# A hybrid encoder layer on one core: MLP operands of the second half in half-width pieces, early operands tied to the softmax, the survey spaced, reciprocal roots on VectorE

## Chip, cores and metric

One core of a Trainium2 chip runs the whole layer in one launch. The metric is device time in microseconds, from start to end of the program. The kernel before took 2134.22 us (median of 3 runs, 2132.43 to 2136.63).

## What is computed

One layer (x is 2048 tokens by 1024 channels, float32):

```python
h = rms_norm(x, norm1_g)
p = h @ w_in                       # 1024 -> 2560, shared by three groups
q, k, v = p[:512], p[512:1024], p[1024:1536]        # 8 heads of 64
q, k = rms_norm(q per head), rms_norm(k per head)
y_attn = softmax(q k^T / 8 + rel_bias) v            # own chunk of 64 and 8 chunks before
y_conv = gb * conv3_causal(gc * hin)                # 256 wide
y_pool = (trailing means over 2, 4, 8, 16 - u) @ pool_w * pool_scale
x = x + concat(y_attn, y_conv, y_pool) @ w_out
h2 = rms_norm(x, norm2_g)
x = x + square(relu(h2 @ w_mlp1)) @ w_mlp2          # 1024 -> 4096 -> 1024
```

The norm of a row is `x * rsqrt(mean(x*x) + 1e-6) * g`. All products are made from a high and a low part of each operand (three matmuls for one), so that float32 accuracy is kept.

## The kernel before, in words

**Four blocks, then two halves.** The first part goes over four blocks of 512 tokens (`block(b, prev_out)`, L374). A block projects q, k and v (`project`, L399), normalizes q and k (`normalize`, L435), and makes the first head pair's operands (`prep`, L453), which are moved by DMA, the keys by way of DRAM (L471, L480, L485), before the first score. Then comes its attention. The second part is the MLP, over two halves of 1024 tokens (`tb` 0 and 1), written as Strassen-like products: seven operands of the data (`OPS`, L329) against seven of the weights (`WORDER`, L49) for each of 64 units (L918). A unit is `up` (L939) or `down` (L965) and has 84 matmuls of 128x512; the order is four up, four down, four times for each half. In the first half the weights' operands are made on ACT, DVE and POOL (`weight_sums`, L812) one unit ahead and kept in DRAM; the second half only loads them (L907).

**Order.** In a block the attention is the main stream, and a side stream is woven into it (`weave`, L75): for every step of the attention 0.95 steps of the side (0.45 in block 0). The PE order is written out by that weaving (`ORDERED`, L44); all other instructions are placed by the framework's scheduler, on each engine and in each DMA queue, by its own timing model: an instruction is put where its inputs are ready and its engine is free, earlier code first. All DMAs go through the SP queue. The side stream (`side`, L770) is the output projection of the block before (`outproj`, L726), its row statistics (`stats`, L746), then the convolution and pooling (`convpool`, L644).

**The survey.** `pace` (L759) also takes a step of the survey (`survey`, L265) at the first two of every five side steps. A survey step issues the loads of two 128x512 tiles of MLP weights and squares, on ACT (L272), the two loaded one step before; four buffers serve them. `paced` (L261) ties a square in the schedule behind the last exponential of the attention that has been written by then; at run time no engine waits for it.

**Early operands.** The first half's seven data operands for each of four `k` (`early_operands`, L331) are made in block 3: 4 loads, 4 DVE products (L347), 7 casts on ACT (L353) with 7 DVE differences (L354), 4 POOL differences (L359 to L368) and 7 stores for each `k`. They need x2 of blocks 0 and 1 only. Their 28 steps stand in `side` behind the statistics, one at each step of `convpool`, and the last ones behind it.

**The second half's operands.** `prepare_spill` (L873) makes them in the MLP's first half, one `k` at each of the units 6, 10, 14 and 18 (`SPILLS`, L48): 2 + 4 loads, 4 DVE products (L869), the sums of `data_sums` (L835, 4 on POOL), 7 casts (L805) and 7 differences (L806), 7 stores (L876). Units 6 and 14 are down units, 10 and 18 up units.

**Roots.** `rsqrt` (L162) is a square root on ACT (L164), a reciprocal on DVE (L166) and one Newton step of four DVE instructions (L168 to L171). It is used three times in a block (rows, q, k) and once for the statistics of each block. The exponential (L549) and the square root need different tables on ACT, and a change of table is an instruction of its own, ACT_TABLE_LOAD.

## Time and profile before

| | |
|---|---|
| runs | 2134.22 us (2132.43 to 2136.63), 3 runs |
| profiled execution | 2131.85 us, span 2130.1 us |
| PE busy | 2040.0 us (96%), 11072 matmuls |
| DVE busy | 1339.8 us (63%) |
| ACT busy | 1019.6 us (48%) |
| POOL busy | 579.0 us (27%) |
| mean DMA rate | 188 GB/s |

The profile is one execution. In the windows view a line is a stretch in us from the span's start; after its length stand the busy time of each engine and the number of its instructions, then the TensorE clock that was granted (1.00 is 2.4 GHz, and a piece at the lower level, 1.2 GHz, counts half), the busy share of the 16 DMA engines and GB/s. In the timeline and the lines view, what stands in brackets or behind the bar is the idle time of that engine just before, and what ended it.

### The profile page before, as it was taken

To read this page: it belongs to the slowest core of one execution; us is meant where nothing else is said; L and a number is where in the kernel's file an instruction comes from. 1 tells how busy PE (TensorE), PEld (TensorE's weight loads), DVE (VectorE), ACT (ScalarE), POOL (GpSimd) and SP (SyncE) were. 2 spreads that over 40 slices of the span, in tenths; PEclk is the share of its full clock that TensorE was granted. 3 is DMA by queue.
4 is the path that set the end of the run, shared out by engine and by line. 5 is a ranking of instruction groups with operands and counts; after the bars stand their busy time and mean duration, and the time that the engine had idled before them with its cause. 6 is when DMAs were issued, how large, how long until landed. Compare 5 with 4: busy or idle time off the path is not lost.

```text
span 2130.1 us, 31726 instructions
## 1 busy us (share of the span) xinstructions
PE 2040.0 (96%) x11072; PEld 1255.2 (59%) x11072; DVE 1339.8 (63%) x2184; ACT 1019.6 (48%) x2036; POOL 579.0 (27%) x441
## 2 busy tenths in 40 slices
PE   8999998999899699999999999999999999999999
PEld 6777787878787588864444444444444444444444
DVE  6776566755679767757768789767743053353354
ACT  5565575747675455535656456356143151150330
POOL 1110012000212213144556456436422031130132
PEclk9999999999999899999999999999999999999999
DMA  9685688648866776483565565548733333333344
GB/s 336 204 258 192 201 270 246 224 139 273 254 211 208 233 209 180 157 327 121 170 221 183 185 201 188 178 160 295 250 116 100 103 101 102 103 95 109 100 152 150
DMA packets 219568, 399.70 MB, mean 188 GB/s; under 512 B 26000, under 2 KB 33296, under 8 KB 219408
## 3 DMA queue, kind: packets, MB, share of 16 engines
q1 hardware_dynamic: 219408, 397.68, 58.3%
q8 instruction: 87, 1.43, 0.3%
q14 instruction: 73, 0.60, 0.1%
HBM read 275.42 MB, written 105.38 MB: 179 GB/s over the span
## 4 chain that ended last, share of the span: by engine, by line
PE 38%; DVE 5%; POOL 3%; DMA 3%; issue 3%; ACT 2%; SPq 0%; POOLq 0%; DVEq 0%; ACTq 0%
PE b_d L855 21%; PE b_u L855 17%; DMA r_d<-w 1%; DVE ft_u L806 1%; POOL t1u L839 1%; DVE a_d L809 1%; DVE acc L976 1%; DVE s_d L809 1%; POOL r_d L824 0%; DVE x L869 0%; POOL s_d L822 0%; DVE a_u L809 0%; DMA rr<-r2d 0%; DMA xd<-yb 0%; ACT ft_u L805 0%
## 5 line engine op out<-in xcount | busy, mean ns | idle before, releaser
L855 PE MATMUL b_d<-ft_u,s_d 128*128 128x512 f16 x1152 | 264.1, 379 | 5.4 <-DVE ft_u L806 2.0
L855 PEld LDWEIGHTS <-s_d 128*128 128x128 f16 x1536 | 150.2, 98 | 188.1 <-issue 7.1
L855 PEld LDWEIGHTS <-s_u 128*128 128x128 f16 x1536 | 150.7, 98 | 186.2 <-issue 7.0
L855 PE MATMUL b_u<-zt,s_u 128*128 128x512 f16 x1152 | 257.3, 381 | 1.8 <-DVE u2u L958 1.0
L976 DVE TENSOR_TENSOR acc<-acc,b_d 128x512 f32<-128x512 f32 x176 | 119.2, 683 | 178.9 <-PE b_d L855 175.6
L855 PEld LDWEIGHTS <-a_u 128*128 128x128 f16 x1152 | 112.7, 98 | 146.3 <-issue 12.7
L855 PEld LDWEIGHTS <-a_d 128*128 128x128 f16 x1152 | 112.7, 98 | 142.5 <-issue 7.4
L855 PE MATMUL b_d<-fb_u,a_d 128*128 128x512 f16 x768 | 183.7, 379 | 3.5 <-DVE fb_u L806 1.7
L855 PE MATMUL b_u<-zb,a_u 128*128 128x512 f16 x768 | 176.6, 379 | 1.3 <-ACT u2u L945 1.3
L839 POOL TENSOR_TENSOR t1u<-u2u,c11u 128x512 f32<-128x512 f32 x32 | 44.0, 1376 | 442.8 <-ACT u2u L962 430.6
L159 PE MATMUL a<-wq,xg 128*128 128x512 f32 x384 | 155.0, 404 | 1.9 <-DVE wq L140 1.8
L158 PE MATMUL a<-wq,xg 128*128 128x512 f32 x384 | 144.6, 403 | 12.5 <-ACT wq L139 12.5
L160 PE MATMUL a<-wq,xg 128*128 128x512 f32 x384 | 153.6, 400 | 0.0
L549 ACT ACTIVATE sb<-sb,nm 128x640 f32<-128x640 f32 (+4 forms) x128 | 97.5, 762 | 110.7 <-DVE nm L543 109.3
L207 POOL TENSOR_TENSOR acc<-acc,sq 128x512 f32<-128x512 f32 x28 | 38.0, 1357 | 379.2 <-ACT sq L206 353.0
L543 DVE CUSTOM_DVE_ANT_0 sb<-s,b 128x640 f32<-128x640 f32 (+4 forms) x128 | 94.3, 737 | 64.6 <-PE s L540 64.0
L562 DVE SCALAR_TENSOR_TENSOR pp<-pt,pp 128x384 f16<-128x384 f32 (+1 forms) x224 | 101.9, 484 | 45.5 <-ACT pp L561 45.0
L139 POOL CAST wc<-rwc 128x512 fp32r<-128x512 f32 x64 | 40.7, 636 | 252.5 <-PE cp L160 109.1
L158 PE MATMUL o<-mix,wo 128*128 128x512 f32 x256 | 106.4, 416 | 1.3 <-ACT mix L641 1.0
L158 PE MATMUL cp<-xg,wc 128*128 128x512 f32 x256 | 106.7, 417 | 0.0
L945 ACT COPY u2u<-b_u 128x512 f32<-128x512 f32 x32 | 18.5, 577 | 179.9 <-PE b_u L855 176.8
L159 PE MATMUL cp<-xg,wc 128*128 128x512 f32 x256 | 101.5, 397 | 0.0
(270 smaller groups left out, 4389.3 us busy)
## 6 DMA issues: line engine op xcount, KB each, us to landing
rwq<-w_qkv SPq DMA_DIRECT2D x96, 256.0 KB, 3.2
p<-w1t SPq DMA_DIRECT2D x64, 256.0 KB, 4.6
rwc<-w_cp SPq DMA_DIRECT2D x64, 256.0 KB, 4.4
rwo<-w_out SPq DMA_DIRECT2D x64, 256.0 KB, 4.0
t<-w SPq DMA_DIRECT2D x64, 256.0 KB, 4.1
r_u<-w SPq DMA_DIRECT2D x64, 256.0 KB, 3.3
wd<-s_u SPq DMA_DIRECT2D x64, 256.0 KB, 2.4
r_d<-w SPq DMA_DIRECT2D x64, 256.0 KB, 3.0
```

The source lines that it names most:

```text
L139: (hi or sc.copy)(w[:, 0], raw)
L158: te.matmul(out, ah, bh, start=start, stop=False)
L159: te.matmul(out, ah, bl, start=False, stop=False)
L160: te.matmul(out, al, bh, start=False, stop=stop)
L207: gp.tensor_tensor(out=acc, in0=acc, in1=q, op=ALU.add)
L543: ve.tensor_tensor_reduce(out=sb[:, :nk].rearrange("p (e k) -> p e k", e=ne), in0=s[:, :ne, :hk], in1=bi[:, 640 - nk :].rearrange("p (e k) ...
L549: exps.append(sc.activation(sb[:, :nk], sb[:, :nk], AF.Exp, bias=nmx, scale=-1.0, accum_out=st["l"][:, i, j : j + 1]))
L562: ve.scalar_tensor_tensor(out=pp[:, 1, c0:c1], in0=pt[:, :n], scalar=PSC, in1=pp[:, 0, c0:c1], op0=ALU.mult, op1=ALU.subtract)
L809: ve.scalar_tensor_tensor(out=t[:, 1], in0=src, scalar=scale, in1=t[:, 0], op0=ALU.mult, op1=ALU.subtract)
L839: gp.tensor_tensor(out=t1, in0=b12, in1=b11, op=ALU.subtract)
L855: te.matmul(bank, w[:, a, q * P : (q + 1) * P], xs[q][:, c], start=start and q == 0 and i == 0, stop=q == n - 1 and i == 2, skip_group_che ...
L976: ve.tensor_tensor(out=a, in0=a, in1=bk, op=ALU.add)
```

## The change

Five edits, in one diff.

- `SPILLS` names eight units, all of them down units: 5 and 7, 12 to 15, 20 and 21. `prepare_spill` makes half of a `k`'s columns at each (256 of each 512), so the four `k` are done in eight pieces; loads, DVE, ACT and POOL instructions are 256 wide, and a store fills half of a row's columns.
- The four DVE products of the early operands are `paced`, as the survey's squares are.
- `side` interleaves the early operands with the whole side stream: one of their steps at each third step from the output projection on; those left over come at its end. The whole stream has 64 steps without them, so 21 of the 28 fall into it and 7 behind it.
- The survey's two steps in five side steps are the first and the fourth, not the first and the second.
- `rsqrt` has a form that needs no ACT: a shift and a subtraction on the integer bits, then three Newton steps of three DVE instructions, 11 in all. The old form stays for the rows, q and k of block 0.

```diff
-SPILLS = (6, 10, 14, 18)
+SPILLS = (5, 7, 12, 13, 14, 15, 20, 21)
...
-    def rsqrt(pool, a, n, tag):
+    def rsqrt_table(pool, a, n, tag):
...
+    def rsqrt(pool, a, n, tag, table=False):
+        if table:
+            return rsqrt_table(pool, a, n, tag)
+        h = pool.tile([P, n], I32, tag=tag + "h", name=tag + "h")
+        ve.tensor_scalar(h, a.bitcast(I32), 1, None, op0=ALU.arith_shift_right)
+        r = pool.tile([P, n], F32, tag=tag + "r", name=tag + "r")
+        ve.tensor_scalar(r.bitcast(I32), h, -1, 0x5F3759DF, op0=ALU.mult, op1=ALU.add)
+        t = pool.tile([P, n], F32, tag=tag + "t", name=tag + "t")
+        for _ in range(3):
+            ve.scalar_tensor_tensor(out=t, in0=r, scalar=-0.5, in1=r, op0=ALU.mult, op1=ALU.mult)
+            ve.tensor_tensor(out=t, in0=t, in1=a, op=ALU.mult)
+            ve.scalar_tensor_tensor(out=r, in0=t, scalar=1.5, in1=r, op0=ALU.add, op1=ALU.mult)
         return r
...
-                    ve.scalar_tensor_tensor(out=t, in0=t, scalar=g2s[:, kk : kk + 1], in1=rr[n], op0=ALU.mult, op1=ALU.mult)
+                    paced(ve.scalar_tensor_tensor(out=t, in0=t, scalar=g2s[:, kk : kk + 1], in1=rr[n], op0=ALU.mult, op1=ALU.mult))
...
-            rstd.append(rsqrt(sm, ms1, NT, "r1"))
+            rstd.append(rsqrt(sm, ms1, NT, "r1", b == 0))
...
-            f = rsqrt(sm, ss.rearrange("p t h -> p (t h)"), NT * H, "rq")
+            f = rsqrt(sm, ss.rearrange("p t h -> p (t h)"), NT * H, "rq", b == 0)
...
         def pace(steps):
             for n, _ in enumerate(steps):
-                if n % 5 < 2:
+                if n % 5 in (0, 3):
                     next(surveyed, None)
...
+        def main_side():
             yield from prev_outproj(weights)
             c = convpool()
             for _ in prev_stats():
                 next(c)
                 yield
+            yield from c
+
+        def side():
             ahead = early_operands() if b == NB - 1 else iter(())
-            for _ in c:
-                next(ahead, None)
+            for n, _ in enumerate(main_side()):
+                if n % 3 == 2:
+                    next(ahead, None)
                 yield
             for _ in ahead:
                 yield
...
-    def prepare(tb, k, mk):
+    def prepare_spill(tb, k, part):
+        cols = slice(256 * part, 256 * part + 256)
...
-                t0 = tb * TM + n * 512
-                t = rp.tile([P, 512], F32, tag="r", name=f"x2_{tb}_{kk}_{n}")
-                sy.dma_start(t, x2d[kk, :, t0 : t0 + 512])
+                t0 = tb * TM + n * 512 + 256 * part
+                t = rp.tile([P, 512], F32, tag="r", name=f"x2_{tb}_{kk}_{part}_{n}")[:, :256]
+                sy.dma_start(t, x2d[kk, :, t0 : t0 + 256])
...
         def mk(src, op):
-            t = split16(src, wp, "w", f"y{op}_{tb}_{k}")
-            sy.dma_start(xd[tb, k, OPS.index(op)], t.rearrange("p a b -> p (a b)"))
+            t = wp.tile([P, 2, 512], F16, tag="w", name=f"y{op}_{tb}_{k}_{part}")[:, :, :256]
+            sc.copy(t[:, 0], src)
+            ve.tensor_tensor(out=t[:, 1], in0=src, in1=t[:, 0], op=ALU.subtract)
+            sy.dma_start(xd[tb, k, OPS.index(op)].rearrange("p (a b) -> p a b", a=2)[:, :, cols], t)
...
-            prepare_spill(1, SPILLS.index(n))
+            prepare_spill(1, *divmod(SPILLS.index(n), 2))
```

## Rows read from the trace of the kernel before

**Rows 1.** The page, span and section 1, whole program.

```profile
span 2130.1 us, 31726 instructions
...
PE 2040.0 (96%) x11072; PEld 1255.2 (59%) x11072; DVE 1339.8 (63%) x2184; ACT 1019.6 (48%) x2036; POOL 579.0 (27%) x441
```

**Rows 2.** Windows, from project to first score, blocks 2 and 3.

```profile
411.60:479.50 67.90, 65.75 (x295) 53.24 (x293) 38.25 (x79) 31.61 (x58) 0.00 (x0) 1.00 0.55 169
646.90:735.60 88.70, 70.30 (x310) 54.99 (x310) 77.10 (x121) 41.66 (x73) 25.58 (x16) 0.93 0.69 220
```

**Rows 3.** Timeline of PE at block 3's first score.

```profile
735.58 0.60 PE L539 MATMUL s<-kx,qs 128*128 128x320 f32 x1 [12.75 <-DMA qs<-qlo]
```

**Rows 4.** Lines, 653 to 742 us, groups of the early operands.

```profile
L347 DVE SCALAR_TENSOR_TENSOR e<-e,g2s,er 128x512 f32<-128x512 f32 x16 | 12.3, 777 | 4.7 <-DMA e<-x2d 2.3 <-DMA er<-r2d 1.9 <-DVE wq L140 0.3
L354 DVE TENSOR_TENSOR et<-e,et 128x512 f16<-128x512 f32 x16 | 11.8, 751 | 6.1 <-ACT et L353 6.1
...
L354 DVE TENSOR_TENSOR eb<-e,eb 128x512 f16<-128x512 f32 x12 | 8.2, 682 | 0.7 <-ACT eb L353 0.7
...
L360 POOL TENSOR_TENSOR e<-e,e 128x512 f32<-128x512 f32 x4 | 7.1, 1777 | 6.9 <-DVE e L347 6.9
```

**Rows 5.** Windows, the attention of blocks 1, 2 and 3.

```profile
246.30:411.60 165.30, 156.24 (x1226) 133.79 (x1227) 112.41 (x230) 113.59 (x289) 26.72 (x29) 0.98 0.80 248
479.50:646.90 167.40, 157.15 (x1210) 133.83 (x1210) 111.34 (x232) 114.86 (x292) 26.36 (x29) 0.97 0.80 249
735.60:889.30 153.70, 152.09 (x1214) 131.81 (x1214) 109.23 (x231) 80.58 (x177) 27.20 (x29) 0.98 0.56 162
```

**Rows 6.** Windows, around the statistics of blocks 0 and 1.

```profile
320.00:345.00 25.00, 18.86 (x149) 16.04 (x148) 16.36 (x35) 13.55 (x31) 5.24 (x6) 0.86 0.83 255
555.00:580.00 25.00, 19.00 (x147) 16.32 (x148) 15.59 (x34) 12.88 (x30) 4.97 (x6) 0.86 0.82 244
```

**Rows 7.** Timeline of ACT, 325 to 334 us.

```profile
330.30 0.63 ACT L272 ACTIVATE p<-p 128x512 f32<-128x512 f32 x1 [4.83 <-DMA p<-w1t]
```

**Rows 8.** Timeline of the SP queue, 320 to 330 us.

```profile
323.58 2.90 SPq L276 DMA_DIRECT2D p<-w1t  x4
```

**Rows 9.** Timeline of PE at 338 us, block 1's attention.

```profile
337.68 0.66 PE L458 MATMUL tq<-ident,nq 128*128 128x128 f32 x2 [3.77 <-DVE klo L463]
```

**Rows 10.** Timeline of ACT, block 2's statistics, in block 3.

```profile
815.69 1.28 ACT L164 ACT_TABLE_LOAD   x1
```

**Rows 11.** Timeline of PE, 819 to 822 us.

```profile
821.62 0.63 PE L458 MATMUL tq<-ident,nq 128*128 128x128 f32 x4 [0.37 <-DVE klo L463]
```

**Rows 12.** Windows in the MLP's first half, each about an up to down change.

```profile
1135.00:1200.00 65.00, 59.08 (x264) 26.02 (x262) 59.35 (x71) 36.85 (x63) 38.20 (x25) 0.97 0.52 175
1200.00:1246.00 46.00, 44.64 (x207) 20.07 (x206) 38.39 (x49) 16.88 (x25) 23.86 (x16) 1.00 0.69 229
1290.00:1345.00 55.00, 48.79 (x222) 21.47 (x220) 50.45 (x57) 33.16 (x58) 36.06 (x24) 1.00 0.47 163
1397.00:1460.00 63.00, 62.62 (x291) 28.27 (x289) 46.82 (x58) 40.39 (x69) 30.59 (x22) 1.00 0.47 162
1460.00:1508.00 48.00, 45.14 (x208) 20.25 (x207) 40.52 (x48) 23.16 (x37) 32.79 (x22) 1.00 0.97 351
```

**Rows 13.** Timeline of DVE, a product of the spill at unit 18.

```profile
1294.38 1.75 DVE L869 SCALAR_TENSOR_TENSOR x<-x,g2s,rr 128x512 f32<-128x512 f32 x1
```

**Rows 14.** Lines by form, DVE, one line at two widths.

```profile
L562 DVE SCALAR_TENSOR_TENSOR pp<-pt,pp 128x256 f16<-128x256 f32 x104 | 43.2, 416 | 1.2 <-ACT pp L561 0.8
L562 DVE SCALAR_TENSOR_TENSOR pp<-pt,pp 128x512 f16<-128x512 f32 x8 | 5.5, 686 | 0.3 <-ACT pp L561 0.3
```

**Rows 15.** One line of the root: min/median/max ns, first and last start.

```profile
L168 DVE TENSOR_TENSOR rqt<-rqr x8: 180/192/906, 49.4 to 706.4; 128x32 f32<-128x32 f32 x8
```

**Rows 16.** Windows before and at the MLP's start.

```profile
850.00:889.00 39.00, 38.06 (x314) 32.51 (x312) 31.74 (x69) 19.74 (x43) 2.55 (x4) 1.00 0.21 61
889.00:912.00 23.00, 22.65 (x102) 17.78 (x103) 15.89 (x22) 10.29 (x17) 7.51 (x5) 1.00 1.03 378
```

More of the change, by code (lines that the diff above doesn't have):

```diff
@@ L171, in rsqrt @@
         ve.tensor_tensor(out=r, in0=r, in1=t, op=ALU.mult)
+        return r
+    I32 = mybir.dt.int32
+    def rsqrt(pool, a, n, tag, table=False):
[10 more added lines that the diff above has]
+            ve.scalar_tensor_tensor(out=r, in0=t, scalar=1.5, in1=r, op0=ALU.add, op1=ALU.mult)
         return r
@@ L768, in block @@
         weights = Ahead(prev_loads + cp_loads)
-        def side():
+        def main_side():
             yield from prev_outproj(weights)
@@ L837, in data_sums @@
         o["b11"] = mk(b11, "b11")
-        t1 = tmp("t1" + nm)
+        t1 = tmp("t1" + nm)[:, : b11.shape[-1]]
         gp.tensor_tensor(out=t1, in0=b12, in1=b11, op=ALU.subtract)
@@ L855, in product @@
                 te.matmul(bank, w[:, a, q * P : (q + 1) * P], xs[q][:, c], start=start and q == 0 and i == 0, stop=q == n - 1 and i == 2, skip_group_check=not start)
-    def prepare(tb, k, mk):
+    def prepare_spill(tb, k, part):
+        cols = slice(256 * part, 256 * part + 256)
         rr = []
         for n in range(2):
-            t = tmp(f"rr{tb}_{k}_{n}")
-            sy.dma_start(t, r2d[2 * tb + n])
+            t = tmp(f"rr{tb}_{k}_{part}_{n}")[:, :256]
+            sy.dma_start(t, r2d[2 * tb + n][:, cols])
             rr.append(t)
@@ L865, in prepare @@
             for n in range(2):
-                t0 = tb * TM + n * 512
-                t = rp.tile([P, 512], F32, tag="r", name=f"x2_{tb}_{kk}_{n}")
-                sy.dma_start(t, x2d[kk, :, t0 : t0 + 512])
+                t0 = tb * TM + n * 512 + 256 * part
+                t = rp.tile([P, 512], F32, tag="r", name=f"x2_{tb}_{kk}_{part}_{n}")[:, :256]
+                sy.dma_start(t, x2d[kk, :, t0 : t0 + 256])
                 ve.scalar_tensor_tensor(out=t, in0=t, scalar=g2s[:, kk : kk + 1], in1=rr[n], op0=ALU.mult, op1=ALU.mult)
                 q.append(t)
-        return data_sums(*q, mk, f"x{tb}_{k}")
-    def prepare_spill(tb, k):
         def mk(src, op):
-            t = split16(src, wp, "w", f"y{op}_{tb}_{k}")
-            sy.dma_start(xd[tb, k, OPS.index(op)], t.rearrange("p a b -> p (a b)"))
-        prepare(tb, k, mk)
+            t = wp.tile([P, 2, 512], F16, tag="w", name=f"y{op}_{tb}_{k}_{part}")[:, :, :256]
+            sc.copy(t[:, 0], src)
+            ve.tensor_tensor(out=t[:, 1], in0=src, in1=t[:, 0], op=ALU.subtract)
+            sy.dma_start(xd[tb, k, OPS.index(op)].rearrange("p (a b) -> p a b", a=2)[:, :, cols], t)
+        data_sums(*q, mk, f"x{tb}_{k}_{part}")
     def reload_steps(tb, out):
```

## The prediction

> **What bounds the kernel now.** I read the page first. PE is busy 2040 of 2130 us [rows 1], so only the time in which PE waits, or runs at the lower clock, is to be had: about 90 us idle, and something for the clock. Next the waits of PE and the windows by stage, to see where that time lies. The MLP's second half is left alone by the change. It touches four places, and in each I compare a stretch that suffers with a like one that does not.
>
> First, block 3's way from projection to first score: 88.7 us against 67.9 us in block 2, with the same matmuls (310 and 295), DVE busy 77.1 us against 38.3, clock 0.93 against 1.00 [rows 2]. PE ends it with one wait of 12.75 us for the first score's operand [rows 3]. The difference in DVE is the early operands: all 16 of their products and all 28 differences lie between 653 and 742 us [rows 4], put there by the scheduler because their inputs were ready and no code held them back.
>
> Second, the attention of blocks 1 and 2 takes 165.3 and 167.4 us, that of block 3, without survey, 153.7 us [rows 5]. In each of the two, one event of 25 us holds most of it: PE busy 18.9 and 19.0, clock 0.86 [rows 6]. It starts on ACT: two squares of the survey stand in its queue before their tiles have landed, 4.83 us [rows 7]; the loads were issued as a run of four only from 323.58 us on [rows 8], after four squares in a row had freed the buffers. The casts behind the squares are late, then DVE's difference of k, and PE waits 3.77 us for it [rows 9].
>
> Third, in the MLP's first half PE waits where up units give way to down units: 5.9 us idle in 1135 to 1200 with clock 0.97, 6.2 us in 1290 to 1345, both just behind a spill in an up unit, DVE busy 91 and 92%; without a spill, 0.4 us in 1397 to 1460 and 2.9 us behind it [rows 12].
>
> Fourth, the start of the MLP, where the DMA engines are full: share 1.03 in 889 to 912 us, after 0.21 in the 39 us before [rows 16].
>
> **The change, part by part.** The sum goes against the profiled execution's own 2131.85 us (span 2130.1 and 1.75 around it); the median of the runs lies 2.4 us above it.
>
> *A, early operands out of block 3's projection.* Each product now comes behind an exponential of block 3's own attention, so none can be placed before the first score. The stretch falls to block 2's length: 88.7 − 67.9 = 20.8 us [rows 2]. The lower clock also reached past the first score (block 3's attention has 0.98 though it hardly waits [rows 5]); I leave that out. Value −21, bounds −22 and −17 (the loads are not held back, and still share the queue).
>
> *B, survey spaced.* At 0.95 side steps for each attention step, 64 side steps fill some 155 us, 2.4 us each. Two survey steps one side step apart leave a load 2.4 us until its square; two or three apart leave 4.8 to 7.3 us, against 4.83 us of lateness here [rows 7]. What it can give is bounded by the events: 25 − 18.9 and 25 − 19.0 = 12.1 us idle, and 14% of 25 us twice = 7 us of clock, together 19 [rows 6]. But the loads were also late because the SP queue had the next heads' operands to issue in front of them [rows 8], and that stays. Value −12, bounds −19 and 0. No other engine's wait takes over at once: block 3 has the same event without a survey, and there PE waits 0.37 us [rows 11].
>
> *C, early operands inside block 3's attention.* 21 of the 28 steps, the operands of three `k`, come there: 12 products, 21 differences, 12 POOL instructions. On DVE, three quarters of what they took before, alone 12.3 + 11.8 + 8.2 = 32.3 us [rows 4], with their effect on others 77.1 − 38.3 = 38.8 us [rows 2]: 24 to 29 us. DVE is busy 109 of 153.7 us in this attention [rows 5], so 44.5 us are free and the work fits, at some 90%. What hides it is DVE's idle time ahead of the scores and transposes; but an instruction of 0.7 us in front of a link of the score chain delays it, and the slack of PE is not in the trace. Bounds 0 (all in gaps) and +29 (every us reaches PE). Nearest is the projection of the same block, where DVE ran at 87% of 88.7 us and PE lost only the waits named above; I take +8. ACT has room (80.6 of 153.7 us, 13 more).
>
> *D, the fourth `k` behind the attention.* Seven steps are written behind everything else, so 4 products and 7 differences, 8 us of DVE, 4 loads and 7 stores of 256 KB come at about 885 to 905 us, where reloads and weights already fill the DMA engines at 378 GB/s [rows 16]: 2.9 MB are 7.6 us. The stores must land before the same tiles are read back, and a wait in the SP queue holds the weight loads behind it. PE has the output projection to do meanwhile. Bounds 0 and +9; I take +3.
>
> *E, half-width pieces in down units.* A spill's 11 DVE instructions cost 4 × 0.78 + 7 × 0.68 = 7.9 us undisturbed, as the like early ones [rows 4]; beside POOL one takes 1.75 us [rows 13]. At 256 columns an instruction is 0.416 us against 0.686 [rows 14], so a piece is 4.6 us and two are 9.2: the whole grows by some 6 us of DVE, on units that have room. Best case: both disturbed changes become like that of 1397 to 1508 (3.3 us): (5.9 + 1.7 + 6.2) − 2 × 3.3 = 7.2 us, and the 1.4 us in 1200 to 1246 goes [rows 12]: −9. But units 12, 13 and 20, 21 are the first down units, in which the last up unit's operands are still being made; DVE stays near full there, and that stretch now has four pieces in a row. Worst case +8, as one more disturbed change. Value −5. SP issues 104 small DMAs for 52; at the 0.7 us of an issue in a crowded stretch [rows 8] that is 36 us more, spread over five stages whose DMA share is 0.47 to 0.69 but for the last [rows 12]: 0.
>
> *F, roots on DVE.* 13 of 16 roots. For 32 columns an instruction is 0.192 us [rows 15]: 11 are 2.1 us against 1.0 us for the old form's five, which also visits ACT. Three times (k of blocks 1 to 3) this lies ahead of the first score. On the other side the change to the root's table and back goes from mid-attention, 1.28 us each way [rows 10]. In block 3 it stood in the same place and PE lost 0.37 us [rows 11], so I give the loads nothing. Value +1, bounds −2 and +5.
>
> Here the Trainium skill would say more. Its page "ScalarE: Activation LUTs", section "Table sets: the hidden batching unit", says that an exponential followed by a square root costs two loads, some 5.3 us with the drains. By it the three pairs in the middle of attentions alone would be worth 3 × 5.3 = 16 us, and the sum 16 us lower; the row of block 3 does not bear that out.
>
> Sum: −21 − 12 + 8 + 3 − 5 + 1 = −26; 2131.85 − 26 = 2105.9, and 2.4 for the median: **2108 us**.
>
> **The rivals.**
>
> *R1, the survey's wait stays (B = 0): 2120 us.* For it: the loads stood behind a run of the SP queue, and spacing leaves those runs where they are. Against it: four squares and four loads in a row are what the old spacing makes. Chance 0.20.
>
> *R2, DVE becomes the bound of block 3's attention: slower, 2155 us.* Mechanism: the 12 POOL instructions there take up to 1.78 us each [rows 4], and a DVE instruction that meets one is held for its length, 1.75 us for 0.78 [rows 4, 13]. The chain of scores runs through DVE twice, so each of the 12 can cost 1.7 us, 20 us in all, on top of the 29 us of bound C. With D at its bound too: −21 − 12 + 49 + 9 − 5 + 1 = +21, so 2131.85 + 21 + 2.4 = 2155. It makes the kernel slower from the point at which the attention grows by some 38 us; it begins where DVE's demand passes the 153.7 us. For it: 109 + 29 + 20 = 158 us. Against it: in the projection the same work met the same POOL instructions and DVE's whole growth was 38.8 us for all four `k`. Chance 0.10. This is what the Trainium skill's page "SBUF — State Buffer", section "Who interferes with whom", would have us fear: a DVE instruction with two inputs in SBUF and a GpSimd instruction take turns, each for the whole of the other. The trace agrees on the holding.
>
> *R3, half of that: the attention grows by 25 to 30 us, and D is 3 to 9: 2125 to 2136 us.* For it and against it what stands under R2. Chance 0.12.
>
> *R4, the pieces move the MLP's waits to the first down units (E = +8): 2121 us.* For it: DVE at 91% there. Against: the piece is smaller than a spill. Chance 0.10.
>
> *R5, the table loads were on the path after all: 2093 us.* ACT loses six loads in mid-attention and as many at the blocks' starts, 12 × 1.28 = 15.4 us, and PE gets all of it. Against it: the 0.37 us. Chance 0.08. The Trainium skill's page "ScalarE: Activation LUTs" stands on this side, as said under F.
>
> *R6, the change doesn't do what it says:* the scheduler puts the early work elsewhere ahead of a first score, A = 0, 2129 us. The tie to the exponential makes that unlikely: within R3's chance.
>
> **How the numbers follow.** Main case 0.40 (2098 to 2118), R1 0.20, R2 0.10, R3 0.12, R4 0.10, R5 0.08. A measurement of this kernel can tell a difference of 0.2%, 4.3 us. Faster than 2129.9: the main case, R1, R4, R5 and a third of R3, less the main case's own tail: 0.79. Slower than 2138.5: R2, 0.10. The rest, 0.11, is the same. The range leaves out R2, the upper part of R3 and the lower part of R5: 2090 to 2130.
>
> **What would show it.** A: the stretch from projection to first score near 69 us in block 3 and no wait over 3 us there; L347 only after the first exponential. B: no ACT wait over 2 us on a survey tile, attention of blocks 1 and 2 at 155 to 160 us. C: block 3's attention at 157 to 167 us with DVE at 85% or more. D: the first MLP matmul up to 8 us later against the end of attention. E: idle PE under 4 us in each of the two disturbed changes. F: two ACT_TABLE_LOADs or so after block 0, at the end. I am wrong if block 3's attention grows by over 25 us, or if the event of rows 6 stays in both blocks.

## The result and the profile after: 0.97% slower

The changed kernel took 2152.93 us (median of 4 runs, 2148.44 to 2157.77) against 2133.32 us (2128.35 to 2136.63, 4 runs) of the kernel before: ratio 1.0097, interval 1.0069 to 1.0124. I had forecast 2108 us, in a range of 2090 to 2130. The profiled execution took 2157.77 us.

The page of after, span and section 1 [rows 1]:

```profile
span 2156.0 us, 31946 instructions
...
PE 2056.1 (95%) x11072; PEld 1262.4 (59%) x11072; DVE 1343.6 (62%) x2306; ACT 1005.3 (47%) x2039; POOL 573.2 (27%) x457
```

PE does the same 11072 matmuls and is busy 16 us longer, partly for a lower clock: the mean granted one is 0.984 against 0.989. The windows of after: from projection to first score of blocks 2 and 3, which answer to [rows 2]; the attention of blocks 1 to 3 [rows 5]; 25 us around each event of [rows 6], which now comes some 10 us sooner in both blocks; and the end of block 3's attention, with [rows 16] as the nearest of before:

```profile
411.80:481.40 69.60, 66.85 (x301) 53.70 (x300) 41.39 (x98) 29.40 (x56) 0.00 (x0) 1.00 0.57 174
646.60:717.00 70.40, 66.77 (x300) 53.59 (x297) 41.33 (x100) 28.25 (x52) 0.00 (x0) 1.00 0.52 162
247.50:411.80 164.30, 157.46 (x1221) 135.15 (x1222) 110.71 (x234) 110.02 (x283) 26.87 (x29) 0.97 0.80 246
481.40:646.60 165.20, 156.59 (x1223) 134.64 (x1223) 111.40 (x235) 110.34 (x284) 26.95 (x29) 0.97 0.79 245
717.00:894.70 177.70, 161.43 (x1215) 136.40 (x1216) 140.12 (x268) 90.34 (x196) 49.76 (x44) 0.94 0.62 188
...
310.00:335.00 25.00, 21.85 (x160) 18.70 (x159) 13.30 (x29) 12.18 (x33) 6.51 (x7) 0.93 0.88 258
545.00:570.00 25.00, 19.23 (x151) 16.60 (x149) 12.82 (x27) 11.03 (x30) 6.58 (x7) 0.86 0.88 262
...
884.00:904.00 20.00, 15.83 (x82) 11.30 (x80) 17.55 (x36) 8.28 (x15) 6.21 (x4) 0.74 0.53 184
```

Block 3's way to its first score fell from 88.7 to 70.4 us, as forecast. Its attention grew from 153.7 to 177.7 us, with DVE at 140 of 177.7 us (79%), PE 16 us idle, where it was 1.6 us, and the clock at 0.94 instead of 0.98. At its end stand 20 us at clock 0.74.

PE's path in the two traces, us from the span's start:

| event | before | after | difference |
|---|---|---|---|
| first score of block 2 | 479.5 | 481.4 | +1.9 |
| first score of block 3 | 735.6 | 717.0 | −18.6 |
| last value of block 3 | 886.9 | 892.3 | +5.4 |
| MLP, 168th matmul | 974.5 | 981.3 | +6.8 |
| MLP, 1512th matmul | 1280.4 | 1300.6 | +20.2 |
| MLP, 2352nd matmul | 1471.3 | 1496.8 | +25.5 |
| end | 2130.1 | 2156.0 | +25.9 |

(The last three lines above the end count the matmuls of the MLP: 84 to a unit, so 2352 are the first 28 units.) So 18.6 us were gained, 24 lost again in the next 175 us, and 19 more in the MLP's first half. The second half is unchanged, as I had said.

**The loss in the attention.** ACT's waits in after, 715 to 897 us (columns: total us, times, longest):

```profile
ACT et L369 <- DMA xd<-et: 10.5, 5, 4.1
ACT et L369 <- DMA xd<-eb: 5.8, 4, 2.6
```

One of them in the timelines of ACT, DVE and PE:

```profile
809.61 0.62 ACT L369 CAST et<-e 128x512 f16<-128x512 f32 x1 [4.09 <-DMA xd<-et]
...
810.26 0.69 DVE L370 TENSOR_TENSOR et<-e,et 128x512 f16<-128x512 f32 x1 [3.42 <-ACT et L369]
813.46 0.68 DVE L479 TENSOR_TENSOR klo<-tk,khi 128x512 fp32r<-128x512 f32 x1
...
814.28 1.09 PE L474 MATMUL tq<-ident,nq 128*128 128x128 f32 x4 [4.74 <-DVE r1t L186]
```

Two buffers serve the early casts. The cast at 809.61 us waits 4.09 us for the store that frees one, and ACT does nothing else meanwhile. DVE stands in front of the difference of that cast for 3.42 us; behind it in DVE's queue stand the first instructions of the new root (some 1.4 us), a score's reduction and the difference of k, and PE waits 4.74 us for those. (The profile names r1t, the last on DVE by then; in [rows 9] the same wait is put down to klo.)

**The loss in the MLP.** From the 168th to the 2352nd matmul, before and then after:

```profile
974.50:1471.30 496.80, 476.90 (x2186) 213.88 (x2185) 391.54 (x466) 276.24 (x463) 267.30 (x179) 1.00 0.55 186
```
```profile
981.30:1496.80 515.50, 484.80 (x2186) 215.63 (x2185) 389.15 (x510) 279.20 (x491) 262.24 (x195) 0.98 0.54 179
```

Of the 18.7 us, PE is idle in 10.8 and longer busy in 7.9, at clock 0.98 for 1.00. The waits in the MLP's first half, of before (1040 to 1530 us):

```profile
PE b_d L855 <- DVE acc L976: 3.0, 3, 1.6
...
DVE x L869 <- DMA x<-x2d: 8.4, 3, 3.5
...
ACT yt L805 <- DMA xd<-yb: 12.8, 7, 2.9
ACT yb L805 <- DMA xd<-yb: 9.4, 2, 4.8
```

The same of after (1052 to 1555 us, the same matmuls):

```profile
PE b_d L875 <- DVE acc L997: 15.6, 6, 4.0
...
DVE x L890 <- DMA x<-x2d: 14.2, 11, 3.7
...
ACT yt L895 <- DMA xd<-yb: 25.4, 13, 4.2
ACT yb L895 <- DMA xd<-yb: 24.3, 5, 6.3
```

DVE's lines of the spill by form, before and then after, 1040 to 1555 us:

```profile
L869 DVE SCALAR_TENSOR_TENSOR x<-x,g2s,rr 128x512 f32<-128x512 f32 x16 | 15.1, 946 | 16.5 <-DMA x<-x2d 8.4 <-DMA rr<-r2d 5.8 <-issue 2.3
...
L806 DVE TENSOR_TENSOR yt<-x,yt 128x512 f16<-128x512 f32 x12 | 14.8, 1239 | 2.6 <-ACT yt L805 2.2
...
L806 DVE TENSOR_TENSOR yb<-x,yb 128x512 f16<-128x512 f32 x12 | 8.2, 681 | 7.0 <-ACT yb L805 7.0
```
```profile
L890 DVE SCALAR_TENSOR_TENSOR x<-x,g2s,rr 128x256 f32<-128x256 f32 x32 | 22.3, 712 | 19.1 <-DMA x<-x2d 14.2 <-DMA rr<-r2d 4.9
L896 DVE TENSOR_TENSOR yt<-x,yt 128x256 f16<-128x256 f32 x24 | 19.2, 802 | 6.4 <-ACT yt L895 6.4
...
L896 DVE TENSOR_TENSOR yb<-x,yb 128x256 f16<-128x256 f32 x24 | 10.4, 448 | 13.5 <-ACT yb L895 13.5
```

And their stores, KB each and us from issue to landing, before and then after:

```profile
xd<-yt SPq DMA_DIRECT2D x16, 256.0 KB, 2.1
xd<-yb SPq DMA_DIRECT2D x12, 256.0 KB, 2.1
```
```profile
xd<-yt SPq DMA_DIRECT2D x32, 128.0 KB, 2.1
xd<-yb SPq DMA_DIRECT2D x24, 128.0 KB, 2.9
```

DVE's work for these operands went from 15.1 + 14.8 + 8.2 = 38 us to 52, and its idle time ahead of them from 26 to 39 us. What stands behind them on DVE can come later for it, the accumulators' updates too, for which PE now waits 15.6 us and before 3.0. That the one makes the other is read from the order of the instructions; it is not shown.

### The profile page after: what moved, and what is told of

The parts are those of the page before. It is cut to its first block, busy times and chain, and to the rows that moved or that the text cites. A ratio compares the mean times of both kernels' runs of the same rounds, so it can differ in the third digit from the quotient of the medians.

```text
span 2156.0 us, 31946 instructions
## 1 busy us (share of the span) xinstructions
PE 2056.1 (95%) x11072; PEld 1262.4 (59%) x11072; DVE 1343.6 (62%) x2306; ACT 1005.3 (47%) x2039; POOL 573.2 (27%) x457
## 4 chain that ended last, share of the span: by engine, by line
PE 61%; DMA 15%; DVE 10%; issue 5%; ACT 4%; POOL 4%; SPq 1%; POOLq 0%; DVEq 0%; ACTq 0%
PE b_d L875 18%; PE b_u L875 18%; PE a L158 4%; PE a L159 4%; PE a L160 4%; DMA r_d<-w 2%; PE cp L158 2%; PE cp L160 2%; PE cp L159 2%; DMA qs<-qhi 2%; DMA x<-x2d 1%; PE pt L576 1%; PE o L158 1%; PE o L159 1%; PE o L160 1%
## 5 line engine op out<-in xcount | busy, mean ns | idle before, releaser
L158 PE MATMUL o<-mix,wo 128*128 128x512 f32 x256 | 109.4, 428 | 3.0 <-DVE m L333 1.5
L139 ACT CAST wq<-rwq 128x512 fp32r<-128x512 f32 x96 | 59.0, 618 | 105.3 <-PE a L160 79.8
L158 PE MATMUL cp<-xg,wc 128*128 128x512 f32 x256 | 107.1, 418 | 0.6 <-DVE ms_2c L230 0.4
L159 PE MATMUL o<-mix,wo 128*128 128x512 f32 x256 | 104.0, 406 | 0.7 <-DVE mix L658 0.7
```

What stands on the lines that cost most here:

```text
L139: (hi or sc.copy)(w[:, 0], raw)
L158: te.matmul(out, ah, bh, start=start, stop=False)
L159: te.matmul(out, ah, bl, start=False, stop=False)
```

## The experiments

Ratios are to the kernel before, timed on the same chip in the same series; the interval is of 95%.

**Each part alone** (pieces, early operands, survey, roots):

```diff
# e1, with the half-width prepare_spill of the change
-SPILLS = (6, 10, 14, 18)
+SPILLS = (5, 7, 12, 13, 14, 15, 20, 21)
# e2, with main_side as in the change
-                    ve.scalar_tensor_tensor(out=t, in0=t, scalar=g2s[:, kk : kk + 1], ...)
+                    paced(ve.scalar_tensor_tensor(out=t, in0=t, scalar=g2s[:, kk : kk + 1], ...))
# e3
-                if n % 5 < 2:
+                if n % 5 in (0, 3):
# e4, with the integer form of rsqrt
-            rstd.append(rsqrt(sm, ms1, NT, "r1"))
+            rstd.append(rsqrt(sm, ms1, NT, "r1", b == 0))
```

> The kernel before with the eight half-width pieces alone. Theory 1 (the pieces cost the MLP its time: DVE and ACT wait in order for a piece's loads and stores, the accumulations behind them come late, PE waits for a bank): about +17 to +20 us against before, up to first score of block 3 nothing changes, and the last attention value comes at the same time. Rival (the loss in the MLP comes from the early operands' late end, which shifts the whole chain): within 3 us of before.

> The kernel before with the early operands paced and interleaved, alone. Theory 1 (ACT waits in order for the stores that free the two buffers of the casts, and holds the attention's casts): first score of block 3 18 to 20 us earlier, its attention 20 to 25 us longer, in all +3 to +8 us. Rival (the roots on DVE, whose chain stood in front of the late difference of k, made half of it): attention only 10 to 14 us longer, in all -6 to -10 us.

> The kernel before with the survey's steps spaced, alone. Theory 1 (the SP queue has the next heads' operands, a store of x2 and the weights in front, so another load is late in the same place): within 4 us of before, with one PE wait of 3 to 6 us in the attention of block 1 and of block 2. Rival (the spacing works and the roots undid it): -10 to -14 us, no PE wait over 2 us there.

> The kernel before with the roots on DVE, alone. Theory 1 (the tables were off the path): within 4 us of before, a little slower rather than faster, with the first score of blocks 1 to 3 1 to 3 us later. Rival (the table loads were on the path): -10 to -15 us.

| run | median us | ratio | interval |
|---|---|---|---|
| e1 pieces | 2146.62 | 1.0049 | 1.0030 to 1.0067 |
| e2 early | 2142.15 | 1.0024 | 1.0008 to 1.0040 |
| e3 survey | 2130.84 | 0.9964 | 0.9949 to 0.9978 |
| e4 roots | 2140.46 | 1.0014 | 0.9999 to 1.0028 |

The pieces (10 us, half of what theory 1 forecast) and the early operands (5 us, as theory 1 forecast) are what costs; the survey's spacing gains 8 us, less than the rival of e3 said and more than its theory 1, whose PE wait stands in both blocks (4.7 us each); the roots give nothing. The parts add up to +0.51%, the whole is +0.97%.

**Why the pieces cost.** Place and width were changed apart (e5, e6), then from the half-width kernel back to whole step by step: slots (e9), loads (e13), and from whole towards half: instructions alone (e14), with their stores (e17), in two rounds (e18).

```diff
# e5, whole width
+SPILLS = (5, 12, 14, 20)
# e6, half width, both pieces of a k in the old unit
+SPILLS = (6, 6.5, 10, 10.5, 14, 14.5, 18, 18.5)
# e9, from e6: two operands in one slot
+            slots.append(slots[-1] if j else wp.tile([P, 2, 512], F16, tag="w", ...))
+            t = slots[-1][:, :, 256 * j : 256 * j + 256]
# e13, from e9: x2d and r2d loaded once, whole
+                sy.dma_start(t, x2d[kk, :, t0 : t0 + 512])
# e14, from before: each instruction of the spill twice
+        parts = [slice(0, 256), slice(256, 512)]
...
+            for c in parts:
+                sc.copy(t[:, 0, c], src[:, c])
# e17, from e14: and each half stored by itself
+                sy.dma_start(xd[tb, k, OPS.index(op)].rearrange("p (a b) -> p a b", a=2)[:, :, c], t[:, :, c])
# e18, whole loads and stores; all instructions of the first 256 columns, then of the others
+        for part in range(2):
+                if part == 1:
+                    sy.dma_start(xd[tb, k, OPS.index(op)], t.rearrange("p a b -> p (a b)"))
```

> The kernel before, with its four whole-width spills moved from units 6, 10, 14, 18 to the down units 5, 12, 14, 20: the place changes, the width does not. The pieces alone (half width, in down units) cost +0.49%, about 10 us. Theory 1, width: two half-width pieces ask for 14 slots of weights, 14 stores and 12 loads where one whole one asks for 7, 7 and 6, and the cast engines wait for them in order; then the place alone costs little: 0.998 to 1.002 of before, waits of TensorE for an accumulator's update (b_d <- acc) about 3 to 6 us. Theory 2, place: in a down unit VectorE also has the twenty-odd accumulator updates, so a spill there delays them whatever its width: 1.004 to 1.010 of before, those waits 12 us or more.

> The kernel before, with each whole spill made as two half-width pieces one right after the other in the same old unit (6, 10, 14, 18): the width changes, the place does not. Theory 1, width (more slots, stores and loads for the same work): 1.004 to 1.009 of before, with more waits of ScalarE for stores (yt, yb <- xd) than before. Theory 2, place: 0.998 to 1.002 of before, since the up units hide it as they hid the whole ones.

> The half-width pieces in the old units (two in each of 6, 10, 14, 18: +0.94% of before, ScalarE waiting 26 us in 4 waits, the longest 9.1 us, for a store to free a buffer) with two operands sharing one weight slot, so that a piece takes 4 slots and not 7; instructions, loads and stores stay. Theory 1, a half-width piece holds full slots until stores that land no sooner than the whole ones (2.5 to 3.0 us for 128 KB against 2.1 for 256 KB) and ScalarE waits in order for them: with 8 slots for 14 the waits of ScalarE on stores fall by half or more and the time to 1.001 to 1.005 of before. Theory 2, the doubled number of instructions, loads and DMA issues costs, whatever the slots: 1.007 to 1.011.

> Half-width pieces in the old units with paired slots (1.0098 of before), but each x2 tile and each root loaded once, whole, for both pieces: 6 loads instead of 12 and 4 raw buffers instead of 8, while instructions and stores stay halved. Theory 1, the doubled loads, which hold raw buffers shared with the weights and land after 2.9 us for 128 KB against 3.5 us for 256 KB: VectorE's waits x <- x2d fall from 18 us to under 10, GpSimd's waits for raw weights from 69 us towards before's 48, time 1.001 to 1.005. Theory 2, the doubled instructions and stores: 1.007 to 1.011.

> The kernel before, whole loads, slots and stores, with only the instructions of the spills cut in two halves of 256 columns, back to back (22 VectorE, 14 ScalarE and 8 GpSimd instructions for 11, 7 and 4). Theory 1, loads and stores are what cost: 0.999 to 1.003 of before. Theory 2, the doubled instructions (by the rows of before 9.2 us of VectorE for 7.9 a spill, and more on ScalarE and GpSimd) cost: 1.005 to 1.011.

> The kernel before with the spills' instructions cut in two halves back to back (1.0012 of before), and now each half stored by itself: 56 stores of 128 KB for 28 of 256 KB. Theory 1, the stores of half rows are what is left of the cost: 1.004 to 1.008 of before. Theory 2, it is the order of the pieces: 1.000 to 1.003.

> The kernel before with whole loads and whole stores, but the spill's instructions in two rounds: first the chain of products, differences and casts of the first 256 columns to its end, then that of the other 256, each operand stored once when both are there. Theory 1 (stores): 1.000 to 1.003 of before. Theory 2, the order: the chain through VectorE, GpSimd and ScalarE is passed twice, and each pass waits for its products in the queues of the weights' work: 1.004 to 1.008.

| run | loads | slots | stores | instructions | ratio | interval |
|---|---|---|---|---|---|---|
| e5, other place | whole | 7 | whole | whole | 0.9991 | 0.9975 to 1.0007 |
| e6 | half | 14 | half | half, two rounds | 1.0094 | 1.0072 to 1.0116 |
| e9 | half | 8 | half | half, two rounds | 1.0098 | 1.0069 to 1.0127 |
| e13 | whole | 8 | half | half, two rounds | 1.0073 | 1.0055 to 1.0090 |
| e14 | whole | 7 | whole | half, back to back | 1.0012 | 1.0001 to 1.0023 |
| e17 | whole | 7 | half | half, back to back | 1.0027 | 1.0012 to 1.0042 |
| e18 | whole | 7 | whole | half, two rounds | 1.0025 | 1.0006 to 1.0043 |

It is the width: whole spills cost nothing in the down units (e5, though PE waits 7.1 us there for accumulators, before 3.0), and half width costs in the old units too. It costs more there, 0.94% against 0.49% of e1, whose eight pieces stand in eight down units and not in pairs; so for half-width pieces the new places were the better ones. ACT's waits for stores in e6, 1040 to 1530 us (before: 12.8 and 9.4 us, longest 4.8):

```profile
ACT yb L875 <- DMA xd<-yb: 25.6, 4, 9.1
ACT yt L875 <- DMA xd<-yt: 12.2, 7, 2.0
ACT yt L875 <- DMA xd<-yb: 8.7, 6, 2.7
```

But sharing the slots, which my first theory took for the cause, changed nothing (e9), though it took these waits from 49 to 23 us. That theory fell. Of the 0.98% of e9, whole loads take back 0.25 (e13); doubled instructions cost 0.12 (e14), half stores 0.15 on top (e17), two rounds 0.13 (e18). These add up to 0.65; the other 0.3 shows only when they come together (e13 against e17 and e18). e17 and e18 were each to show that the other's part was the cause, and both came out small. No single one is shown to be the cause: the shares of 0.12 to 0.25 are about as large as their uncertainty, or smaller. And what is taken apart here is e6, with its pieces in pairs; the 0.49% of the change's own places was not taken apart.

**Why the early operands cost.**

```diff
# e7, from e2: a step for each put
-                if n % 3 == 2:
+                if n % 3:
# e8, from e2
+                third = OPS.index(op) % 3 == 2
-                t = scr.tile([P, 2, 512], F16, tag="pg", bufs=2, name=f"e{op}_{k}")
+                t = scr.tile([P, 2, 512], F16, tag="x" if third else "pg", bufs=3 if third else 2, ...)
# e10, from e8: the four differences of a k
-            gp.tensor_tensor(out=b11, in0=b12, in1=b11, op=ALU.subtract)
+            ve.tensor_tensor(out=b11, in0=b12, in1=b11, op=ALU.subtract)
# e11, from e8
+                    if k >= 2:
+                        paced(m)
# e12, from the change: prepare_spill and SPILLS as before
# e15, from e11
-                if n % 3 == 2:
+                if n % 2:
# e16, from e15
+                if n % 5 in (0, 3):
```

> The early operands interleaved and paced as in the run that changed them alone (+0.24%, attention of block 3 171 us instead of 151), but with one split and store per step, in two of three side steps, so that no two stores of one step stand behind one another and nothing is left after the attention. Theory 1, ScalarE waits in order for the store that frees a cast buffer and everything behind it in ScalarE and VectorE is late: those waits (et <- xd and eb <- xd) fall from 14 us to under 6, block 3's attention to 158 to 165 us, the time to 0.994 to 0.999 of before. Theory 2, the work itself on VectorE and GpSimd in that attention is what costs: attention 168 to 174 us, time 1.000 to 1.004 of before.

> The early operands interleaved and paced as in the run that changed them alone, with every third split going to a buffer of another set of three, so that five buffers instead of two stand between a cast and the store it waits for; the steps stay as they were. Theory 1, waits for store buffers: ScalarE's waits for xd fall from 14 us to under 4, block 3's attention from 171 to 158 to 166 us, time 0.994 to 1.000 of before. Theory 2, the work itself or the order of the loads on SP's queue costs: waits gone but attention still 168 to 174 us, time 1.001 to 1.004 of before.

> The early operands interleaved and paced with the five cast buffers (1.0011 of before; block 3's attention 168.5 us), and their four differences per k made on VectorE and not on GpSimd. Theory 1, GpSimd's instructions of 1.6 to 1.8 us hold VectorE's two-input instructions (1.75 us in place of 0.7 beside them): GpSimd falls back to some 27 us busy in block 3's attention, VectorE's busy time there, 138.9 us, does not grow by the 16 x 0.6 = 9.6 us added, the attention is 160 to 166 us and the time 0.996 to 1.000 of before. Theory 2, it is VectorE's own work in front of the chain of scores that costs: VectorE some 145 us busy, attention 170 to 176 us, time 1.001 to 1.004.

> The early operands interleaved, five cast buffers, but only the products of the third and fourth k are tied to the softmax; those of the first two are free to be placed as early as the scheduler will, as all were before. So about half of the work lies in block 3's projection and half in its attention. Theory 1, the cost in either place grows more than in proportion, because TensorE waits only when bursts on VectorE outlast its slack: stretch from projection to first score 70 to 78 us, attention 156 to 161 us, sum 4 to 10 us under before's 240, time 0.995 to 0.998 of before. Theory 2, each operand costs the same in either place (17 to 21 us for four k in each): the sum stays within 3 us of 240 and the time at 0.999 to 1.002.

> The change without the half-width pieces: early operands, survey and roots as changed, spills as before. The parts alone were +0.24% (early), -0.36% (survey), +0.14% (roots) and +0.49% (pieces), together +0.51%, while the whole was +0.97%. Theory 1, the parts add up and the excess is scatter between runs: 0.999 to 1.002 of before. Theory 2, the early operands and the survey meet in block 3 and cost more together: 1.004 to 1.007. Theory 3, the excess comes with the pieces, since the MLP starts later in the change and the weights' loads run otherwise against them: 0.999 to 1.002 too, and then the excess is not settled by this run alone.

> The early operands half in the projection, half in the attention (0.9999 of before), with a step at every second side step instead of every third, so that the last k ends inside the attention. Theory 1, the tail behind the attention costs (1.0 to 1.6 us waits in a row and 10.24 us at the lower clock, some 8 to 10 us in all, which before does not have): no piece of 10 us at the lower clock behind the last values, last output projection 4 to 8 us sooner than in the run it follows, time 0.995 to 0.998. Theory 2, the work only meets the chain of scores instead: attention 164 to 170 us in place of 160, time 0.999 to 1.002.

> The same with the survey's steps spaced as in the change (alone 0.9964 of before). If the parts add up, as their places do not meet (the survey is over before block 3's attention): 0.992 to 0.996 of before, the fastest so far, and 0.4% or less below the kernel it follows. If the early operands without a tail gain nothing: 0.996 to 0.999.

In us, for one profile each, from the last value of block 2 to the first score of block 3, from there to the last value, and the sum:

| run | to score | attention | sum | ratio | interval |
|---|---|---|---|---|---|
| before | 88.0 | 151.3 | 239.3 | 1 | |
| e2 | 71.5 | 171.2 | 242.7 | 1.0024 | 1.0008 to 1.0040 |
| e7, one split a step | 72.0 | 176.0 | 248.0 | 1.0051 | 1.0034 to 1.0069 |
| e8, five cast buffers | 71.8 | 168.5 | 240.3 | 1.0011 | 0.9994 to 1.0028 |
| e10, differences on DVE | 72.1 | 168.4 | 240.5 | 1.0033 | 1.0017 to 1.0048 |
| e11, half in the projection | 73.9 | 160.0 | 233.9 | 0.9999 | 0.9985 to 1.0014 |
| e12, change without pieces | 71.3 | 173.7 | 245.0 | 1.0032 | 1.0012 to 1.0052 |
| e15, e11 without tail | 73.6 | 162.6 | 236.2 | 0.9991 | 0.9976 to 1.0006 |
| e16, e15 and survey | 74.7 | 162.1 | 236.8 | 0.9968 | 0.9951 to 0.9984 |

(In ten other kernels that leave the early operands as before the sum is 237.2 to 241.8 us.) e7 fell outside both of its theories: ACT's waits for stores in block 3's attention rose from 14 to 23 us, and the attention by 5. e8 took them from 14 to 8 us, and the attention lost only 2.7 of its 20 us: the waits are a part of the loss; what the 8 us that stayed still cost was not tested. What else stands ahead of the scores is seen in e8's DVE timeline, 846 to 857 us, and PE's there:

```profile
846.89 0.68 DVE L140 TENSOR_TENSOR wc<-rwc,wc 128x512 fp32r<-128x512 f32 x1
847.50 1.75 DVE L695 SCALAR_TENSOR_TENSOR yc<-z,col,yc 128x512 f32<-128x512 f32 x1
849.16 0.81 DVE L544 CUSTOM_DVE_ANT_0 sb<-s,b 128x640 f32<-128x640 f32 x1
...
852.50 1.09 DVE L355 TENSOR_TENSOR eb<-e,eb 128x512 f16<-128x512 f32 x1
853.52 0.68 DVE L355 TENSOR_TENSOR et<-e,et 128x512 f16<-128x512 f32 x1
854.12 1.76 DVE L700 TENSOR_TENSOR yc<-yc,gb 128x512 f32<-128x512 f32 x1
855.81 0.81 DVE L544 CUSTOM_DVE_ANT_0 sb<-s,b 128x640 f32<-128x640 f32 x1
...
850.04 0.43 PE L540 MATMUL s<-kx,qs 128*128 128x320 f32 x1 [2.65 <-DVE nm L544]
```

DVE has no gap in these 10 us. The reduction of a score (L544), on which PE's next score waits, stands behind early differences and behind two-input instructions of 1.75 us, of which the like take 0.7 where no GpSimd instruction of 1.6 us runs beside them. DVE is busy 139 of 168.5 us over the attention, but in this profile it has five stretches of 10 to 35 us without a gap over 0.3 us, and before has one of 14 us. In e10 GpSimd's differences were moved to DVE:

```profile
717.20:885.60 168.40, 156.55 (x1211) 132.94 (x1211) 136.54 (x269) 90.77 (x196) 28.51 (x29) 0.97 0.64 197
```

POOL is at 28.5 us for 49, DVE's busy time did not grow with the added instructions (136.5 us for 139), and yet the attention is the same. So GpSimd's holding of DVE costs DVE as much as making the differences itself, and taking it away did not shorten the attention. But ACT's waits for stores rose in e10 from 8 to 11 us, the longest to 6.3, so that a small gain can be hidden. Theory 1 had the busy time right, theory 2 the time. That the amount of DVE work ahead of the scores is the rest of the cause is argued from what is left over; ACT's own casts and the early loads and stores in SP's queue were not taken out apart. The Trainium skill's page "SBUF — State Buffer", section "Who interferes with whom", made me fear the holding; the trace agrees with it, the price is another matter. With half of the work in each place (e11) the sum falls by 5 us, as was forecast for a cost that grows faster than the work. But it does so in the projection alone, which is 2.4 us longer with half of the work there and 16.5 with all of it (73.9 and 88.0 against 71.5); the attention is 8.7 us longer with half and 17.2 with all (e8), in proportion. And the medians show none of the 5 us (0.9999); the MLP of that profile is 6 us longer than that of before, and no run shows why.

e12 is 0.3% above the sum of its three parts (+0.02%), and the pieces add 0.65% to it where alone they were 0.49%. That is 0.3 with an uncertainty of about the same size; whether the parts hinder each other, I leave open.

e16 beats both kernels: 0.9968 of before. e3 with 0.9964 does as much with one edit, so the early operands' new place is worth nothing that these runs can tell. e15 did take away the stretch at the lower clock behind the attention (its row stands with the hardware below), but its last output projection ended at 951 us, not sooner than e11's 945: the attention is 2.6 us longer, and it began 2.2 us later.

## Why the prediction was wrong, by its own steps

- **A, −21: right.** The first score came 18.6 us sooner and the stretch has block 2's length.
- **B, −12: a part of it.** The spacing alone gave −8 us (e3, 5 to 11). The waits on survey tiles went (4.83 us [rows 7]; the longest in after is 1.4 us). The events stayed, smaller in block 1 (21.9 us busy of 25, clock 0.93) and whole in block 2 (19.2 us, clock 0.86). PE now waits there for work behind another late load, in the timelines of DVE and PE in block 2:

```profile
552.37 0.69 DVE L140 TENSOR_TENSOR wc<-rwc,wc 128x512 fp32r<-128x512 f32 x1 [8.69 <-POOL wc L139]
...
553.58 0.69 PE L576 MATMUL pt<-ident,sb 128*128 128x128 f32 x2 [5.77 <-DVE pp L578]
```

  The loads of rwc were issued from 545.13 us on, behind nine DMAs of a head's operands, the survey and a store, issued one after another. In block 1, and in both blocks of e3, DVE and PE wait in the same way (PE 3.2, 4.7 and 4.7 us). That is R1's ground, the crowded SP queue; I had named it and given it 0.20, and by my own sign, the event in both blocks, I was wrong. The attentions of blocks 1 and 2 together take 328.0, 329.5, 325.2 and 330.7 us in the four profiles with the new spacing and 332.6 in the mean of fifteen with the old one: −4. (e4, with the old spacing and the roots on DVE, has 328 too, so after's share of the 4 is not told apart.)
- **C, +8: the step that failed first.** From the first score to the last value it was 24 (from −18.6 to +5.4); e2, which holds A, C and D alone, gives +5 us in the medians, so C and D are some 24 there too. I priced the work on DVE as a whole (109 + 29 of 153.7 us) and took the projection as the nearest row, as if the work had cost PE little there. My own A had it at 21 us there, of which three quarters are 16. DVE's load came out lower than I said, 79% for 85% or more, and the cost three times as high, so the mean load of DVE does not set it. Two things were missed. ACT's casts wait for stores; in before's projection the same waits stand (12.4 us for casts of et behind stores of eb alone), and I had not listed them. e8 shows them to be a part of the loss. And the attention passes DVE for every score, so that PE waits where DVE is full for a stretch, whatever its mean; this second part is argued from e8's timelines.
- **D, +3: +1.4 behind the last value** (from +5.4 to +6.8). Its steps show as the 20 us at clock 0.74, a part of which lies ahead of the last value and so in C's 24. My sign for it failed: the first MLP matmul comes 27.6 us after the last value and not 12.6, but by the 168th only 1.4 us are left.
- **E, −5: the wrong sign, +10 alone and +14 in the change.** e1 gives 10 us (6 to 14), after against e12 0.65%, 14 us, and the profiles 19. My bound was +8. I took 6 us more of DVE and "units that have room"; it was 14 us more of work and 13 more of waiting ahead of that work on DVE. I had counted SP's issues and set the extra DMAs to 0. A store of half the bytes lands after 2.1 to 2.9 us, against 2.1 for the whole, so more waits came with half the work each. The Trainium skill, in "DMA: Bandwidth & Descriptors", section "Latency and other measured facts", gives a DMA a fixed cost of about 2 us, mostly the way to memory and back. The trace agrees, and I had not weighed that sentence against the diff. Which of loads, stores, instructions and order costs how much stays open (e9 to e18).
- **F, +1: right in size.** 1.0014, 3 us, not clear of nothing, and ACT_TABLE_LOADs fell from 16 to 4. R5 falls, and with it the sum by the Trainium skill's "ScalarE: Activation LUTs", section "Table sets: the hidden batching unit": 12 loads fewer gained PE nothing that can be measured.
- **The rivals.** R2 had the time (2155) by luck, not the way there. Its price was on the attention alone, +49 with bound C, where 24 came; it had DVE full with 158 us of demand, and DVE was busy 140; and its mechanism, POOL holding DVE, was taken away in e10 without a gain. R3, the attention 25 to 30 us longer, was nearest for the attention, and R4 was right in kind for the pieces, with a price of +8 for the 10 to 14 that came. No rival had both.
- **The profiled executions.** The 25.9 us between the two profiles are 6 more than the 19.6 between the medians: after's profiled execution lies 4.8 us above its median, and before's 1.5 us below. Before's MLP took 1155.6 us from the 168th matmul; eleven other kernels with whole spills and whole instructions took 1158.0 to 1164.4. Against their mean, 1161, E is +13 and not +19.
- **What stays open.** The parts alone add up to 11 us (5.1 − 7.7 + 10.5 + 3.0) and the whole is 20. Where the other 9 come from is not shown, and their uncertainty is nearly as large.

## What to carry to other kernels

Before moving work to stand ahead of a critical chain in an engine's queue, list every wait the moved instructions have now, and ask what will stand behind each of them in the new place. The engine's mean load does not price such work: here some 30 us of work on DVE at 79% load cost 24 us. Halving the size of a step that loads and stores halved neither its DMAs' time nor its waits here: move the whole step, which cost nothing (e5), before trying to halve it.

## What the runs showed of the hardware

Short waits of PE in a row, and its clock. Where the fourth `k` comes at the end of block 3's attention, PE in after waits 1.46, 0.86, 0.22, 0.89 and 0.68 us between 888 and 899 us, and in this stretch the granted clock falls to the lower level, 1.2 GHz: the mean is 0.74 in 884 to 904 us (above). In e15, in which that tail is gone, it is 1.00 at the same place:

```profile
880.00:900.00 20.00, 18.70 (x115) 14.17 (x113) 13.18 (x30) 9.51 (x16) 2.88 (x2) 1.00 0.73 253
```

Half the columns are not half an instruction: the spill's DVE instructions fell from 0.946 to 0.712 us, from 1.239 to 0.802 and from 0.681 to 0.448, to between 65 and 75% (rows above). A store of half the bytes took no less: 2.1 and 2.9 us for 128 KB, 2.1 us for 256 KB.
